# Tile sums of the Down projection made from whole SwiGLU tiles read back from DRAM, and two more paired slabs

## The chip, the cores and the metric

One core of a Trainium2 chip runs the kernel. The metric is device time in microseconds. The kernel before takes 1428.65 us (median of 3 runs, 1428.42 to 1428.69). Its parts: TensorE (PE) multiplies matrices and accumulates in PSUM; VectorE (DVE), ScalarE (ACT) and GpSimd (POOL) do the elementwise work; SyncE (SP) and POOL issue most of the DMA transfers between DRAM and the on-chip memory (SBUF). Each engine works through its own queue in order, so an instruction that waits holds up all that stands behind it on that engine.

## The reference

One encoder block on a sequence of 256 tokens with a model width of 2048, all in float32. The input is normalised and sent through four mixers, whose outputs go through one projection; cross-attention to 256 memory rows follows; then comes the SwiGLU feed-forward part, which is where the change lies:

```
x = x + mix @ w_out
x = x + cross_attention(rms_norm(x, norm_g[1]), mem_n, w_xq, w_xkv, w_xo)
def swiglu(h, w_gate_up, w_down):
    gate, up = jnp.split(h @ w_gate_up, 2, axis=-1)
    return (jax.nn.silu(gate) * up) @ w_down
x = x + swiglu(rms_norm(x, norm_g[2]), w_gate_up, w_down)
return rms_norm(x, final_norm_g)
```

The hidden width is 5632, that is 44 tiles of 128. `w_gate_up` is 2048 x 11264 and `w_down` 5632 x 2048.

## The kernel before

**Precision.** A float32 product is made of three matmuls in a faster format. Each operand is split into a high and a low half (`wh` and `wl` for weights, the two halves of a 512-wide tile for activations), and high x high, high x low and low x high are added up. `part` (lines 472 to 474) issues these three, each 512 columns wide. ScalarE makes the high half by a copy that rounds, VectorE the low half by a subtraction.

**Weights.** `Stream` reads the weights from DRAM in slabs of 128 x 2048 values, in the order of use. SyncE loads a slab into one of a few `raw` buffers; ScalarE and VectorE split it, in pieces ("halves"), into one of a few pairs `wh`/`wl`. In Down there are three `raw` buffers and four such pairs, so the split can run ahead of TensorE by some three pieces. `_plain` (lines 166, 167) splits a plain slab in two pieces of 1024. The splits of consecutive slabs keep their order by explicit dependencies.

**Paired slabs.** For some slabs (`S` in a plan string) the kernel uses Strassen's scheme as Winograd arranged it, on blocks of two tiles of the contracted dimension, two column blocks and the two halves of the rows: seven products in place of eight. A plain slab is 8 calls of `part`, a paired one 7. In return it needs sums of weights and sums of activations. `_sums` (lines 178, 179, 189) makes the weights' part: pieces of 1024, 512, 1024 and 1024, and between the second and the third either four additions of 512 on VectorE, or, for "summed" slabs, two, after SyncE has loaded a part, ScalarE has copied it (line 119) and a DMA from POOL that adds (line 121) has made the rest in one of the four `res` tiles. Only gate_up's paired slabs are summed. Down's make the four additions.

**Sums of activations.** `combine` makes, for a pair of activation tiles `a`, `b`, the sums of their row halves and splits them into a tile `z` (in Down: `y0` to `y7`). The tiles lie in SBUF in split form, so it first adds high and low halves again (two additions of 128 x 256), then makes four sums of 128 x 128, then splits them. In Down with its narrower `y` tiles the fourth sum overwrites the first tile of the pair. A pair's sums are made once; pass two uses those of pass one again.

**gate_up.** Eleven groups of 512 hidden columns. The first is plain; the plans `GROUPS` hold for the other ten: nine times `NSSNSSNN`, and `NSNSNSNN` for the last. After a group the SwiGLU product is transposed and stored by POOL to a DRAM tensor, `hidden` (`self.ff`; line 600). `load_turned` (line 605) loads a tile of it back in the arrangement that Down needs: 128 KB in runs of 128 bytes, issued by POOL. `fetch` loads tiles and splits them into `f`: 22 early ones during gate_up, the other 22 (`rest`, running six loads ahead of the splits) from the last group on. Tiles 20 to 27 of `f` lie in the buffers `z` of gate_up's own sums, tiles 28 to 43 in those of its input. At the end the `res` tiles, which held weight sums, get the residual back from DRAM (line 1230).

**Down.** Two passes over 22 slabs, each for two blocks of 512 output columns, with the plans `PASSES`. In pass one the plain slabs take `soon` tiles first. `ready(k)` drives the fetch so that the tile of a step is there, at a pace of three tiles in four steps. The generator `combined` calls `combine` for one pair after another; `before(j)` drives it, so that the sums of slab j have been issued when slab j begins. `mixed` and `done` add the products to the residual; `mixed` uses a 128 x 512 tile `u`. The last 12 steps are held back for `down_end`.

**Order.** `Background` is a planner at build time. Generators such as `fetch` and `combined` do a piece and yield a pause; `poll`, called after every part, resumes those whose pause has passed on a clock that counts 0.68 us for a part, but only while the planner's tally of VectorE's debt (`owed`) is under 0.9 us. The debt is added to the pause. `keep_place` ties an instruction to its place on its engine's queue.

Of the kernel before, what the change touches and what calls it, by code (L numbers as in the profile page):

```python
# [49 lines left out]
PAIRED = {a + i for a, plan in [(GATE_UP + 8 * j, GROUPS[j % len(GROUPS)]) for j in range(10)] + [(DOWN, PASSES[0]), (DOWN + 22, PASSES[1])]  # L50
          for i, x in enumerate(plan) if x in "Ss"}
AHEAD = (-3, -3)

SUMS = [{GATE_UP + 8 * j + i + a: GATE_UP + 8 * j + i for j in range(10) for i, x in enumerate(GROUPS[j % len(GROUPS)]) if x == "S"}
        for a in AHEAD]

SUMMED = {GATE_UP + 8 * j + i for j in range(10) for i, x in enumerate(GROUPS[j % len(GROUPS)]) if x == "S"}

# [18 lines left out]
class Stream:  # L77


    def __init__(self, tc, pools, W, bg):  # L80
        self.tc, self.nc, self.W, self.bg = tc, tc.nc, W, bg
        self.rawp, self.wp = pools
        self.order = []
        self.n = self.made = 0
        self.after = []
        self.halves = []
        self.at = self.phase = 0
        self.raw = None
# [6 lines left out]
        self.begun = []  # L95

# [8 lines left out]
    def _load(self, n):  # L105
# [4 lines left out]
        self.raw = slot[0].tile([P, 2048], F32, name="raw", tag="raw")  # L110
        if n // 16 in SUMS[0]:
            t = self.sums[0]
            self.sums.append(self.sums.pop(0))
            nc.sync.dma_start(t[:, 0:512], self.W[SUMS[0][n // 16]][:, 1536:2048])
            self.begun.append(t)
        if n // 16 in SUMS[1]:
            t = self.begun.pop(0)
# [3 lines left out]
            nc.gpsimd.dma_start(t, self.W[SUMS[1][n // 16]][:, 512:1536], accum_op=ALU.add)  # L121
            self.two.append(t)
# [170 lines left out]
class Block:  # L293
# [563 lines left out]
    def whole(self, c):  # L857
        return self.res[c].rearrange("p k r -> p (k r)")

    def leave(self, c):  # L860
        self.nc.sync.dma_start(self.rd[:, c * 1024:(c + 1) * 1024], self.whole(c))
# [238 lines left out]
    def gate_up(self, gp, f, z):  # L1100
# [39 lines left out]
        def fetch(k0, k1, ahead, pause, after=0, slow=False):  # L1140

            m = {}
            for k in range(k0, k1 + ahead):
# [11 lines left out]
                if k >= k0 + ahead:  # L1155
                    while k0 == 0 and k - ahead >= 20 and "free" not in box:
                        yield
                    mark = self.mark()
# [47 lines left out]
        up(0, ps[1])  # L1206
        early = fetch(0, FT - 22, 2, 2.0, 12, True)
        self.bg.drain(comb)
        for j in range(1, DFF // 512):
            plan = GROUPS[(j - 1) % len(GROUPS)]  # L1210
            if j == 10:
                box["free"] = True
# [15 lines left out]
        more.close()  # L1228
        for c, x in enumerate(whole):
            nc.sync.dma_start(x, self.rd[:, c * 1024:(c + 1) * 1024])  # L1230
        for _ in early:
# [3 lines left out]
    def down(self, f, sp):  # L1235
# [8 lines left out]
        u = sp.tile([P, 512], F32, name="u")  # L1244
        sums = [((2 * i, 2 * i + 1), z[i % 8]) for i in range(PASSES[1].count("S"))]
# [41 lines left out]
        def ready(k):  # L1287

            need = min(FT, max(k + 3, FT - 22 + next(asked) * 3 // 4))
            while self.have < need:  # L1290
                self.bg.step(next(e for e in self.bg.q if e[0] is self.fetch))

        for i, plan in enumerate(PASSES):
            n = plan.count("S")
# [697 lines left out]
```

## Time and profile before

The profiled execution took 1428.43 us; its span from the first to the last instruction is 1426.6 us.

| | busy us | share of the span |
|---|---|---|
| TensorE matmul | 1416.5 | 99% |
| TensorE weight load | 1176.1 | 82% |
| VectorE | 1174.3 | 82% |
| ScalarE | 850.2 | 60% |
| POOL | 243.4 | 17% |

The granted TensorE clock is 0.999 of full speed over the span. The last gate_up group runs from about 1146 us to 1186 us of the span; Down's first pass begins at 1186.42 us, where TensorE first reads a tile `f`. Matmuls are pipelined: a record of 0.39 us begins before the one ahead of it ends, so the pitch from start to start tells the throughput, not the length.

### The profile page before, as it was taken

What the parts mean: (1) busy time and instruction counts of PE and PEld (TensorE: products, weight loads), DVE (VectorE), ACT (ScalarE), POOL (GpSimd) and SP (SyncE); (2) the same over time, 40 slices, a digit from 0 to 9 for tenths busy, and PEclk for the clock granted to TensorE, in tenths of its full rate; (3) what the DMA queues carried; (4) which work ended last, traced back from release to release, by engine and by line L of the source; (5) the groups of instructions that cost most, each with busy time, mean ns of one, the idle gap of its engine ahead of it and who ended that gap; (6) DMA issues with size and microseconds to landing.
All of it is one profiled execution on the core that took longest, in us unless ns stands there. A gap on an engine that the chain in (4) does not pass through costs nothing.

```text
span 1426.6 us, 18663 instructions
## 1 busy us (share of the span) xinstructions
PE 1416.5 (99%) x6562; PEld 1176.1 (82%) x6562; DVE 1174.3 (82%) x1782; ACT 850.2 (60%) x1242; POOL 243.4 (17%) x315
## 2 busy tenths in 40 slices
PE   9999999999999999999999999999999999999997
PEld 8888888888888888888888888888888888788886
DVE  6667868787878767677578999999999988989997
ACT  7566665445755555555465676667666665655655
POOL 0000100003212233531331121122211024000000
PEclk9999999999999999999999999999999999999999
DMA  9886554457566797965798999999999898665554
GB/s 356 294 291 250 204 198 174 161 177 232 183 216 215 234 278 249 276 197 188 252 298 257 265 280 283 288 291 260 278 291 273 276 276 242 212 235 179 193 220 148
DMA packets 72462, 344.84 MB, mean 242 GB/s; under 512 B 10894, under 2 KB 12591, under 8 KB 45745
## 3 DMA queue, kind: packets, MB, share of 16 engines
q1 hardware_dynamic: 52976, 285.31, 57.4%
q0 software_dynamic: 18960, 57.69, 17.2%
q8 instruction: 51, 0.84, 0.2%
q10 hardware_dynamic: 432, 0.66, 0.1%
q14 instruction: 43, 0.34, 0.1%
HBM read 321.07 MB, written 22.54 MB: 241 GB/s over the span
## 4 chain that ended last, share of the span: by engine, by line
PE 92%; issue 3%; DVE 2%; DMA 2%; POOL 1%; ACT 0%; SPq 0%; DVEq 0%; ACTq 0%; POOLq 0%
PE pg L472 21%; PE pg L474 21%; PE pg L473 21%; PE pm L473 6%; PE pm L474 6%; PE pm L472 6%; PE pg L420 4%; PE pg L421 2%; PE pm L1445 1%; DMA raw<-in_W 1%; PE pm L1074 1%; DMA tmp<-hidden 1%; POOL tmp L605 1%; PE pm L1045 1%; DVE wl L179 0%
## 5 line engine op out<-in xcount | busy, mean ns | idle before, releaser
L167 DVE TENSOR_TENSOR wl<-raw,wh 128x1024 fp32r<-128x1024 f32 (+1 forms) x395 | 473.7, 1212 | 161.3 <-ACT wh L166 159.4
L166 ACT CAST wh<-raw 128x1024 fp32r<-128x1024 f32 (+1 forms) x395 | 406.4, 1042 | 253.0 <-PE pg L474 189.0
L472 PE MATMUL pg<-wh,act 128*128 128x512 f32 (+1 forms) x1165 | 455.5, 391 | 0.0
L474 PE MATMUL pg<-wh,act 128*128 128x512 f32 (+1 forms) x1165 | 453.9, 390 | 0.5 <-DVE act L322 0.5
L473 PE MATMUL pg<-wl,act 128*128 128x512 f32 (+1 forms) x1165 | 453.6, 389 | 0.2 <-DVE wl L167 0.2
L474 PEld LDWEIGHTS pg<-wh,act 128*128 128x128 f32 x1165 | 218.9, 188 | 47.0 <-DVE act L322 1.1
L472 PEld LDWEIGHTS pg<-wh,act 128*128 128x128 f32 x1165 | 219.0, 188 | 46.8 <-issue 1.5
L473 PEld LDWEIGHTS pg<-wl,act 128*128 128x128 f32 x1165 | 219.0, 188 | 45.1 <-DVE wl L167 0.5
L178 ACT CAST wh<-raw 128x1024 fp32r<-128x1024 f32 (+1 forms) x177 | 161.5, 918 | 158.8 <-DVE raw L189 62.7
L179 DVE TENSOR_TENSOR wl<-raw,wh 128x1024 fp32r<-128x1024 f32 (+1 forms) x177 | 182.7, 1057 | 25.7 <-ACT wh L178 24.3
L473 PE MATMUL pm<-wl,act 128*128 128x512 f32 x290 | 112.9, 389 | 0.2 <-DVE wl L167 0.2
L472 PE MATMUL pm<-wh,act 128*128 128x512 f32 x290 | 112.8, 389 | 0.0
L474 PE MATMUL pm<-wh,act 128*128 128x512 f32 x290 | 112.8, 389 | 0.0
L420 PE MATMUL pg<-act,wh 128*128 128x512 f32 x256 | 90.5, 395 | 0.0
L121 POOL DMA_DIRECT2D res<-in_W x39 | 35.0, 897 | 238.3 <-ACT res L119 211.1
L421 PE MATMUL pg<-act,wl 128*128 128x256 f32 x256 | 71.8, 280 | 0.0
L189 DVE TENSOR_TENSOR raw<-raw 128x512 f32<-128x512 f32 x99 | 68.2, 689 | 1.6
L473 PEld LDWEIGHTS pm<-wl,act 128*128 128x128 f32 x290 | 54.4, 188 | 11.8 <-DVE wl L167 0.5
L474 PEld LDWEIGHTS pm<-wh,act 128*128 128x128 f32 x290 | 54.4, 188 | 11.3
L472 PEld LDWEIGHTS pm<-wh,act 128*128 128x128 f32 x290 | 54.4, 188 | 11.3
L420 PEld LDWEIGHTS pg<-act,wh 128*128 128x128 f32 x256 | 48.1, 188 | 10.5
L178 ACT CAST wh<-res 128x1024 fp32r<-128x1024 f32 x39 | 41.2, 1055 | 14.8 <-PE pg L474 4.1
(376 smaller groups left out, 1933.0 us busy)
## 6 DMA issues: line engine op xcount, KB each, us to landing
raw<-in_W SPq DMA_DIRECT2D x207, 1024.0 KB, 5.5
raw<-in_W SPq DMA_DIRECT2D x39, 768.0 KB, 8.9
res<-in_W POOLq DMA_DIRECT2D x39, 512.0 KB, 9.7
res<-in_W SPq DMA_DIRECT2D x39, 256.0 KB, 4.9
raw<-in_W SPq DMA_DIRECT2D x11, 512.0 KB, 7.1
hidden<-g POOLq DMA_DIRECT2D x22, 256.0 KB, 4.0
tmp<-hidden POOLq DMA_DIRECT2D x44, 128.0 KB, 10.5
features<-tmp POOLq DMA_DIRECT2D x32, 128.0 KB, 4.6
```

Source lines behind the costliest of these rows:

```text
L121: nc.gpsimd.dma_start(t, self.W[SUMS[1][n // 16]][:, 512:1536], accum_op=ALU.add)
L166: nc.scalar.copy(wh[:, a:b], r[:, a:b])
L167: nc.vector.tensor_tensor(out=wl[:, a:b], in0=r[:, a:b], in1=wh[:, a:b].bitcast(F32), op=ALU.subtract)
L178: nc.scalar.copy(wh, src)
L179: nc.vector.tensor_tensor(out=wl, in0=src, in1=wh.bitcast(F32), op=ALU.subtract)
L189: nc.vector.tensor_tensor(out=out, in0=a, in1=b, op=ALU.add)
L420: self.nc.tensor.matmul(p[:, :], wh, slot[:, :], start=start, stop=False)
L421: self.nc.tensor.matmul(p[:, 0:R], wl, slot[:, 0:R], start=False, stop=stop)
L472: self.nc.tensor.matmul(p, hi, wh, start=start, stop=False)
L473: self.nc.tensor.matmul(p, hi, wl, start=False, stop=False)
L474: self.nc.tensor.matmul(p, lo, wh, start=False, stop=stop)
L605: self.nc.gpsimd.dma_start(t.rearrange("p (g t) -> p g t", t=32), src)
```

## The change

- Down's `combine` no longer adds the split halves. For each pair two DMAs from POOL load the whole tiles from `hidden` into the two halves of `u`, and `combine` reads those. `u` holds one pair at a time: the loads of a pair are issued when the pair before is combined, and the generator then pauses 10 us on the planner's clock. The first loads of a pass are issued as it begins. `combine` needs two temporary tiles, not four.
- `before(j)` asks for the sums of the pair of slab j+1 when slab j begins, so a plain slab lies between.
- The plans: the last gate_up group is like the others (four pairs, not three), and pass one of Down has seven pairs, not six, the first at slabs 5 and 7 (were 5 and 8). Down's paired slabs are now spelled `s`; as before they are not summed by DMA.
- As the last group now uses all four `z`, 20 tiles are fetched early, not 22, and 24 in `rest`, which runs seven loads ahead, starts one step earlier in the last group, and is paced by five tiles in eight steps. Pass one's `soon` tiles are 14 to 19 (were 12 to 19).
- `begins` replaces the table `SUMS`; with these plans it gives each sum the same place, three slabs ahead. `fetch_rows` is the loop of line 1230 under a name.

```diff
+EARLY = 20
-GROUPS = *["NSSNSSNN"] * 9, "NSNSNSNN"
+GROUPS = "NSSNSSNN",
-PASSES = "NNNNNSNNSNNSNSNNSNNSNN", "NSNSNSNSNSNSNSNSNSNNNN"
+PASSES = "NNNNNsNsNNsNsNNsNsNsNN", "NsNsNsNsNsNsNsNsNsNNNN"
...
+def begins():
+    at = {}
+    ns = sorted(SUMMED)
+    for i, n in enumerate(ns):
+        a = max(n - 3, ns[i - 4] + 1) if i >= 4 else n - 3
+        assert a not in at and a < n, (a, n)
+        at[a] = n
+    return at
...
-    def combine(self, z, a, b):
-        tt, t, u, v, w = self.tt, *(self.tmp() for _ in range(4))
-        for x, y in ((t, a), (u, b)):
-            tt(x, y[:, 0:R].bitcast(F32), y[:, R:512].bitcast(F32), ALU.add)
-        yield SOON
+    def combine(self, z, a, b, whole=None):
+        tt = self.tt
+        if whole:
+            t, u, v, w = *whole, self.tmp(), self.tmp()
+        else:
+            t, u, v, w = (self.tmp() for _ in range(4))
+            for x, y in ((t, a), (u, b)):
+                tt(x, y[:, 0:R].bitcast(F32), y[:, R:512].bitcast(F32), ALU.add)
+            yield SOON
...
-        early = fetch(0, FT - 22, 2, 2.0, 12, True)
+        early = fetch(0, EARLY, 2, 2.0, 12, True)
...
-                rest = fetch(FT - 22, FT, 6, SOON, slow=True)
+                rest = fetch(EARLY, FT, 7, SOON, slow=True)
...
-                if j == 10 and i > 2:
+                if j == 10 and i > 1:
                     next(rest)
...
         def combined(n):
-            for ks, x in sums[len(made):n]:
-                yield from self.combine(x, *(f[k] for k in ks))
+            whole = [u[:, a:a + R] for a in (0, R)]
+            todo = sums[len(made):n]
+            def load(ks):
+                mark = self.mark()
+                for y, k in zip(whole, ks):
+                    self.load_turned(y, self.ff, k)
+                self.keep_place(mark)
+            load(todo[0][0])
+            yield 10.0
+            for i, (ks, x) in enumerate(todo):
+                yield from self.combine(x, *(f[k] for k in ks), whole)
                 made.append(x)
-                yield 2.0
+                if i + 1 < len(todo):
+                    load(todo[i + 1][0])
+                    yield 10.0
...
-            need = min(FT, max(k + 3, FT - 22 + next(asked) * 3 // 4))
+            need = min(FT, max(k + 3, EARLY + next(asked) * 5 // 8))
...
-            g = self.bg.add(combined(n))
+            g = self.bg.add(combined(n), go=True)
...
             def before(j):
-                while plan[j] == "S" and len(made) <= plan[:j].count("S"):
+                while len(made) < sum(x in "Ss" for x in plan[:j + 2]):
                     self.bg.step(next(e for e in self.bg.q if e[0] is g))
...
-                                        () if i else range(2 * n, 2 * n + 8))
+                                        () if i else range(2 * n, EARLY))
```

More of the change, by code (lines that the diff above doesn't have):

```diff
@@ L42 @@
 LATE = 12
+EARLY = 20
 GATE_UP = 1920 // 16 + 8
-GROUPS = *["NSSNSSNN"] * 9, "NSNSNSNN"
+GROUPS = "NSSNSSNN",
 DOWN = GATE_UP + 80
-PASSES = "NNNNNSNNSNNSNSNNSNNSNN", "NSNSNSNSNSNSNSNSNSNNNN"
[L50 to L57, printed above, removed]
+PASSES = "NNNNNsNsNNsNsNNsNsNsNN", "NsNsNsNsNsNsNsNsNsNNNN"
+PLANS = [(GATE_UP + 8 * j, GROUPS[j % len(GROUPS)]) for j in range(10)] + [(DOWN, PASSES[0]), (DOWN + 22, PASSES[1])]
+PAIRED, SUMMED = ({a + i for a, plan in PLANS for i, x in enumerate(plan) if x in kinds} for kinds in ("Ss", "S"))
+def begins():
[6 more added lines that the diff above has]
+    return at
+SUMS = begins()
 LAG, OWED, SOON, FAR = 1.3, 0.9, 0.01, 18.0
@@ L94, in __init__ @@
         self.two = []
-        self.begun = []
     def _buffers(self, n, m):
@@ L110, in _load @@
         self.raw = slot[0].tile([P, 2048], F32, name="raw", tag="raw")
-        if n // 16 in SUMS[0]:
+        if n // 16 in SUMS:
             t = self.sums[0]
             self.sums.append(self.sums.pop(0))
[L114 to L117, printed above, removed]
+            nc.sync.dma_start(t[:, 0:512], self.W[SUMS[n // 16]][:, 1536:2048])
             mark = len(nc.cur_bb.bb.instructions)
@@ L120, in _load @@
             self.keep(mark)
-            nc.gpsimd.dma_start(t, self.W[SUMS[1][n // 16]][:, 512:1536], accum_op=ALU.add)
+            nc.gpsimd.dma_start(t, self.W[SUMS[n // 16]][:, 512:1536], accum_op=ALU.add)
             self.two.append(t)
@@ L858, in whole, with fetch_rows @@
         return self.res[c].rearrange("p k r -> p (k r)")
+    def fetch_rows(self, cs):
+        for c in cs:
+            self.nc.sync.dma_start(self.whole(c), self.rd[:, c * 1024:(c + 1) * 1024])
     def leave(self, c):
@@ L1155, in fetch @@
                 if k >= k0 + ahead:
-                    while k0 == 0 and k - ahead >= 20 and "free" not in box:
-                        yield
                     mark = self.mark()
@@ L1228, in gate_up @@
         more.close()
-        for c, x in enumerate(whole):
-            nc.sync.dma_start(x, self.rd[:, c * 1024:(c + 1) * 1024])
+        self.fetch_rows(range(4))
         for _ in early:
@@ L1244, in down @@
         u = sp.tile([P, 512], F32, name="u")
-        sums = [((2 * i, 2 * i + 1), z[i % 8]) for i in range(PASSES[1].count("S"))]
+        sums = [((2 * i, 2 * i + 1), z[i % 8]) for i in range(sum(x in "Ss" for x in PASSES[1]))]
         made, split = [], []
         def combined(n):
-            for ks, x in sums[len(made):n]:
-                yield from self.combine(x, *(f[k] for k in ks))
+            whole = [u[:, a:a + R] for a in (0, R)]
[9 more added lines that the diff above has]
+                yield from self.combine(x, *(f[k] for k in ks), whole)
                 made.append(x)
-                yield 2.0
+                if i + 1 < len(todo):
+                    load(todo[i + 1][0])
+                    yield 10.0
         def squares(x, c, r):
@@ L1293, in down @@
         for i, plan in enumerate(PASSES):
-            n = plan.count("S")
-            g = self.bg.add(combined(n))
+            n = sum(x in "Ss" for x in plan)
+            g = self.bg.add(combined(n), go=True)
             late = (0, LATE)[i]
```

2 lines of the change are left out of this document (removed).

## The prediction

> **What bounds the kernel now.** I read the page first (busy times, chain), then TensorE's waits, then a table of stretches, then the timelines around the two places where TensorE stops.
>
> ```profile
> span 1426.6 us, 18663 instructions
> PE 1416.5 (99%) x6562; PEld 1176.1 (82%) x6562; DVE 1174.3 (82%) x1782; ACT 850.2 (60%) x1242; POOL 243.4 (17%) x315
> PE 92%; issue 3%; DVE 2%; DMA 2%; POOL 1%; ACT 0%; SPq 0%; DVEq 0%; ACTq 0%; POOLq 0%
> ```
>
> TensorE is busy in 99% of the span and carries 92% of the chain that ended last. A shorter time needs fewer matmuls, or fewer stops. This is all that TensorE waits for:
>
> ```profile
> PE pm L643 <- DVE eps L644: 1.1, 1, 1.1
> PE pg L474 <- DVE act L322: 0.5, 1, 0.5
> PE pm L472 <- ACT y L338: 0.2, 1, 0.2
> PE pg L473 <- DVE wl L167: 0.2, 1, 0.2
> PE pm L473 <- DVE wl L167: 0.2, 1, 0.2
> ```
>
> Only the first row lies outside the stages that the change touches: it is the start. The next view is the table of stretches; its columns are the stretch and its length, then busy time with instruction counts for PE, PEld, DVE, ACT and POOL, the granted clock, the DMA share and GB/s. The first row is ordinary gate_up groups, the second the last group, and Down's first pass runs from 1186 to about 1301.
>
> ```profile
> 900.00:1000.00 100.00, 100.00 (x443) 82.81 (x442) 96.35 (x119) 66.12 (x82) 20.13 (x23) 1.00 0.94 280
> 1146.00:1186.00 40.00, 40.00 (x179) 33.10 (x178) 33.86 (x39) 22.62 (x26) 6.96 (x8) 1.00 0.87 259
> 1186.00:1213.00 27.00, 27.00 (x121) 22.36 (x120) 22.25 (x36) 14.96 (x25) 15.57 (x18) 1.00 0.89 241
> 1213.00:1241.00 28.00, 27.27 (x119) 21.86 (x118) 27.27 (x51) 18.40 (x29) 0.88 (x1) 1.00 0.74 241
> 1241.00:1270.00 29.00, 29.00 (x130) 24.01 (x129) 28.93 (x56) 16.30 (x26) 0.00 (x0) 1.00 0.55 207
> 1270.00:1301.00 31.00, 31.00 (x139) 25.66 (x138) 26.07 (x36) 17.11 (x20) 0.00 (x0) 1.00 0.48 172
> ```
>
> VectorE is the second bound: 22.25 + 27.27 + 28.93 + 26.07 = 104.5 us of the 115 of pass one, and nearly all of 1213 to 1270. That TensorE loses so little shows that the split weights lie ahead of it in their buffers. A new stop therefore comes from VectorE or ScalarE falling behind by more than that lead.
>
> **Step 1: two products fewer.** Counted from the strings, pair slabs go from 9x4 + 3 + 6 + 9 = 54 to 40 + 7 + 9 = 56. A plain slab is 8 parts of three matmuls, a pair slab 7. The pitch of a part:
>
> ```profile
> 1186.42 0.39 PE L472 MATMUL pg<-wh,f 128*128 128x512 f32 x1
> 1188.46 0.39 PE L472 MATMUL pg<-wh,f 128*128 128x512 f32 x1
> ```
>
> These are the first matmuls of parts 1 and 4 of Down: 2.04 us for three parts, 0.68 each (0.39 is the pipelined length of one). Two parts are **-1.36 us**, certain as long as TensorE stays the bound. Plain and pair slabs then take 5.44 and 4.76 us.
>
> **Step 2: the stops that a late combination makes.** The two stops of the first pass:
>
> ```profile
> 1214.98 0.48 PE L472 MATMUL pg<-wh,act 128*128 128x512 f32 x1
> 1215.71 0.47 PE L472 MATMUL pm<-wh,y 128*128 128x512 f32 x1 [0.25 <-ACT y L338]
> 1231.46 0.39 PE L474 MATMUL pg<-wh,act 128*128 128x512 f32 x1
> 1232.33 0.50 PE L474 MATMUL pg<-wh,act 128*128 128x512 f32 x1 [0.48 <-DVE act L322]
> 1232.67 0.40 PE L472 MATMUL pm<-wh,y 128*128 128x512 f32 x1
> ```
>
> Both wait for results of `combine` (`y`, and its fourth sum, written back into `act`): slab 5 and slab 8, the first two pair slabs. The starts should be 0.227 apart, so they cost 0.50, and 0.64 + 0.11, some **1.27 us** with the matmul behind the first stop. Now `before(j)` asks for the pair of slab j+1 before slab j begins, so these results are a plain slab early. I take -1.27; the ends are 0 and -1.27. The two stops late in pass two (0.2 each in the waits) stand where no combination is made, so I leave them; at best they go too, 0.4.
>
> **Step 3: VectorE's sum.** The durations, from the groups of VectorE between 1186 and 1301:
>
> ```profile
> L179 DVE TENSOR_TENSOR wl<-raw,wh 128x1024 fp32r<-128x1024 f32 x18 | 22.0, 1221 | 4.2 <-ACT wh L178 4.1
> L189 DVE TENSOR_TENSOR raw<-raw 128x512 f32<-128x512 f32 x24 | 16.5, 687 | 0.2
> L322 DVE TENSOR_TENSOR act<-tmp,act 128x256 fp32r<-128x256 f32 x16 | 6.4, 420 | 0.6 <-ACT act L330 0.6
> L322 DVE TENSOR_TENSOR tmp<-tmp 128x128 f32<-128x128 f32 x24 | 6.2, 285 | 0.1
> L179 DVE TENSOR_TENSOR wl<-raw,wh 128x512 fp32r<-128x512 f32 x6 | 4.1, 688 | 1.1 <-ACT wh L178 1.1
> ```
>
> A pair slab in Down is 3 x 1.22 + 0.69 + 4 x 0.69 = 7.1 us, a plain one 2 x 1.22 = 2.44. A combination was 2 x 0.42 (the adds now gone) + 4 x 0.285 + 0.42 + 2 x 0.285 = 3.0; it becomes 2.1. Pass one: one more pair slab +4.7, 6 x 3.0 becoming 7 x 2.1 = -3.3, two more tiles to split (24 for 22) +0.84, so +2.2: 106.7 of 114.3 us, 93%. The mean has room. Pass two makes two combinations in place of three: 9.0 becomes 4.2, no cost. In the last group a summed pair slab has two adds: 3 x 1.22 + 0.69 + 2 x 0.69 = 5.7 for 2.44, so 33.9 + 3.3 = 37.2 of 39.3, the 95% at which the groups of 900 to 1000 run without a stop: 0. Its added SyncE and POOL loads and ScalarE copy are those of one more such slab, as in the groups before; it ends, like them, in two plain slabs. All four residual tiles now wait for that group's sums, so on SyncE one reload more may stand ahead of weight loads, as this one does without TensorE stopping: 0.
>
> ```profile
> 1168.74 0.33 SPq L1230 DMA_DIRECT2D res<-residual  x1
> 1206.15 0.43 DVE L322 TENSOR_TENSOR act<-tmp,act 128x256 fp32r<-128x256 f32 x1 [0.56 <-ACT act L330]
> ```
>
> Locally it is tighter. The first pair slabs are 5 and 7 (were 5 and 8), with one plain slab between. The second row is VectorE's last idle gap before the stops, 20 us into Down. Slab 7 starts at 5 x 5.44 + 4.76 + 5.44 = 37.4, and its last sum is read 3.4 later, at 40.8. In the 20.8 us between, VectorE owes two pair slabs, one plain, combination 1 and some five tile splits: 14.2 + 2.4 + 2.1 + 2.1 = 20.8. Back-to-back instructions overlap a little, so the isolated durations overstate. The margin is that of a pair-plain-pair run in pass two:
>
> ```profile
> 1330.62 1.23 DVE L179 TENSOR_TENSOR wl<-raw,wh 128x1024 fp32r<-128x1024 f32 x1
> 1332.92 0.39 PE L473 MATMUL pm<-wl,act 128*128 128x512 f32 x1
> ```
>
> The low half of the pair slab's last sum ends at 1331.85, TensorE reads it at 1332.92: 1.07 us. A combination of 2.1 us inside such a run overdraws it by at most 1.0. In the old first pass a 3.0 us combination beside slabs 11 and 13 cost nothing (no wait there). I take **+0.5** for slab 7, +0.2 for slabs 12, 17 and 19 together; ends 0 and 4 x 1.0.
>
> **Step 4: eighteen new loads on POOL.** Nine pairs need two whole tiles each from `hidden` into the two halves of `u`. The rows of the like loads, in POOL's timeline, the source's landing times and ScalarE's timeline:
>
> ```profile
> 1191.20 7.03 POOL L605 DMA_DIRECT2D tmp<-hidden  x8
> 1209.07 0.88 POOL L605 DMA_DIRECT2D tmp<-hidden  x1 [0.94 <-DVE act L322]
> 1215.10 0.88 POOL L605 DMA_DIRECT2D tmp<-hidden  x1 [5.15 <-DVE tmp L322]
> DMA to landing us min/median/max: 5.2/10.6/13.1
> 1198.20 0.41 ACT L330 CAST z<-tmp 128x256 fp32r<-128x256 f32 x1 [2.37 <-DMA tmp<-hidden]
> ```
>
> The first pair's loads go ahead of the tile loads and push them back by 2 x 0.88 = 1.76 us. ScalarE already waits 2.37 there at no cost to TensorE, and one more tile is loaded early in the last group (six for five), so 0. The first combination reads 10 us and VectorE's debt after its loads are emitted; POOL is free for them at 1191.2, 5 us into Down, and a first load there lands 7 us on (1191.20 to 1198.20), while VectorE is idle in part: 0. Pair 1 is the delicate one: its loads stand behind a dozen tile loads, which come in one per some 1.4 us (the first at 1198.20, the sixteenth, issued at 1209.07, at about 1219.7 by the median). As loads 15 and 16 they land 32 to 34 us into Down. VectorE wants them at 32 to 33: the demand falls before slab 6, 5 x 5.44 + 4.76 = 32.0 in. Its subtract blocks VectorE in order: behind it wait the low halves of slab 7, and TensorE for those. I take +0.2, as the two instants nearly meet; ends 0 and +7 (all tile loads ahead of it: the old ones are in at 1215.10 + 5.2 = 1220.3, five more make 1226 to 1227, 40 us into Down and 7 late). Later pairs load alone; the one old load so placed (1215.10) is at the minimum, 5.2, so with 1.76 of issue they fit into 10: 0. A POOL load into `u` waits for the subtracts before it; behind it wait tile loads, seven tiles ahead of use now.
>
> [...]
>
> **The sum.** -1.36 - 1.27 + 0.7 + 0.2 = -1.73. The profiled execution took 1428.43 (span 1426.6 and 1.8 around it), 0.22 below the median of 1428.65; to the median I forecast **1426.9 us**, -0.12%. About 0.2% (2.9 us) is what a measurement of this kernel can tell from no change.
>
> **Rivals.** *A: every stop goes.* Both stops of step 2 and the two late ones go (-1.36 - 1.27 - 0.4), nothing new: 1425.6. For it: pass two has one combination less and 5 us less VectorE work. Against: the late stops lie beside the final additions, not beside a combination.
>
> *B: VectorE stops TensorE at each pair-plain-pair.* Slabs 7, 12, 17 and 19 lose 1.0 each: 1428.65 - 2.63 + 4.0 = 1430.0, the saving given back. For it: the margin of 1.07, and VectorE at 93% in the mean. Against: the old slabs 11 and 13.
>
> *C: the tiles come late for every pair.* If the loads keep the crowded landing time of 10.6 even after the fetch is over, each pair is 10.6 + 1.76 - 10 - 1.07 = 1.3 us late at TensorE, and six pairs make 7.8: 1428.65 - 2.63 + 7.8 = 1433.8, slower by 0.36% (the end of +7 in step 4 would give 1433.5 with the 0.5 of step 3). It decides against the kernel from a landing time of about 10.2 on (5.5 us over six pairs). Against it stands the 5.2 of the lone load. [...]
>
> *D: the parts are saved but not felt*, because VectorE already sets the pace. The page has TensorE at 99% against 82%; it could only be so inside pass one, which is B.
>
> **How the numbers follow.** My forecast 0.50 (its own range 1425.8 to 1428.2), A 0.12, B with D 0.23, C 0.15. The range, 1425.4 to 1431.0, holds all but C and a few hundredths of the tails of A and B. Faster by over 0.2% (below 1425.8) is most of A: 0.10. Slower (above 1431.5) is C and the tail of B: 0.16. Within: 0.74.
>
> **What would show it.** Lines 472 to 474 hold two matmuls fewer each. No TensorE wait on `y` or `act` near 1215 and 1232; the late ones still there. POOL has 18 loads `u<-hidden` and no idle of 5 us before its last tile load. VectorE is 2 us busier in pass one and 5 less in pass two. A VectorE wait on the load into `u` just before slab 7 is my delicate place; one before every pair, with TensorE waiting on `wl`, is C and would make the prediction wrong. Stops at slabs 7, 12, 17 and 19 with no wait on a load are B.

## The result, and the profile after

The changed kernel takes 1442.05 us (median; 1441.5 to 1442.7). The kernel before, run beside it, takes 1428.67 us (1428.42 to 1429.41). The ratio is 1.0093, with a 95% interval of 1.0075 to 1.011. The forecast of 1426.9 us is wrong, in sign and by more than its range: the kernel is slower by 13.4 us.

The profiled execution took 1442.7 us. First the top of its page, with busy times by engine and the chain's shares:

```profile
span 1440.9 us, 18712 instructions
PE 1420.9 (99%) x6556; PEld 1177.2 (82%) x6556; DVE 1176.9 (82%) x1774; ACT 854.0 (59%) x1247; POOL 259.9 (18%) x334
PE 94%; DMA 2%; DVE 1%; issue 1%; POOL 1%; ACT 0%; SPq 0%; DVEq 0%; POOLq 0%; ACTq 0%
```

Six matmuls fewer (6556 for 6562) are the two products saved. Yet TensorE is "busy" 4.4 us longer: its matmuls take longer somewhere. What TensorE waits for (total, times, longest):

```profile
PE pg L478 <- DVE wl L184: 3.8, 1, 3.8
PE pg L479 <- DVE act L327: 3.3, 1, 3.3
PE pm L477 <- ACT wh L183: 2.0, 1, 2.0
PE pm L478 <- DVE wl L184: 1.1, 1, 1.1
```

These four rows are new, and all are paired-slab work (L184 and L183 split the pieces of a paired slab, L327 is the two-input operation of `combine` and of the tile splits). The table of stretches tells where, with the same columns and stretches as before:

```profile
1146.00:1186.00 40.00, 40.00 (x178) 33.12 (x177) 36.08 (x41) 24.69 (x27) 7.84 (x9) 1.00 0.94 292
1186.00:1213.00 27.00, 27.00 (x121) 22.34 (x120) 18.55 (x32) 13.20 (x23) 16.44 (x19) 1.00 0.88 262
1213.00:1241.00 28.00, 21.14 (x83) 16.42 (x82) 23.20 (x38) 14.91 (x23) 7.05 (x8) 0.88 0.64 184
1241.00:1270.00 29.00, 25.68 (x101) 20.41 (x100) 23.04 (x44) 15.32 (x26) 4.40 (x5) 0.88 0.47 163
1270.00:1301.00 31.00, 30.98 (x137) 25.19 (x136) 29.01 (x45) 17.20 (x24) 1.76 (x2) 1.00 0.65 239
```

Nearly all of the loss lies in the third and the fourth row, slabs 5 to 12 of Down's first pass: 83 and 101 matmuls where there were 119 and 130. The last gate_up group, with its fourth pair, is full (40.00 of 40). VectorE is not overloaded in the two bad stretches: it does less than before (23.20 for 27.27, 23.04 for 28.93). It stands still. Its timeline (start, length, instruction, and in brackets the idle time before it and what ended that):

```profile
1209.76 0.41 DVE L327 TENSOR_TENSOR act<-tmp,act 128x256 fp32r<-128x256 f32 x1
1217.51 0.49 DVE L327 TENSOR_TENSOR tmp<-u 128x128 f32<-128x128 f32 x2 [7.34 <-DMA u<-hidden]
...
1218.45 0.68 DVE L184 TENSOR_TENSOR wl<-raw,wh 128x512 fp32r<-128x512 f32 x1
...
1247.74 0.29 DVE L327 TENSOR_TENSOR tmp<-u 128x128 f32<-128x128 f32 x1 [3.32 <-DMA u<-hidden]
```

For 7.34 us VectorE stands at the second pair's tiles, and for 3.32 us at the fourth's. Queued behind is the second piece of slab 5's weights (128x512), which was due long before that pair's sums are. TensorE's timeline, around the two places:

```profile
1215.03 0.39 PE L477 MATMUL pg<-wh,act 128*128 128x512 f32 x1
1219.19 0.50 PE L478 MATMUL pg<-wl,act 128*128 128x512 f32 x1 [3.77 <-DVE wl L184]
...
1221.88 0.80 PE L477 MATMUL pm<-wh,y 128*128 128x512 f32 x1 [1.96 <-ACT wh L183]
1223.80 0.80 PE L478 MATMUL pm<-wl,y 128*128 128x512 f32 x1 [1.13 <-DVE wl L184]
1224.39 0.63 PE L479 MATMUL pm<-wh,y 128*128 128x512 f32 x1
1224.82 0.63 PE L477 MATMUL pm<-wh,y 128*128 128x512 f32 x1
...
1252.04 1.22 PE L479 MATMUL pg<-wh,act 128*128 128x512 f32 x2 [3.31 <-DVE act L327]
1253.06 0.63 PE L477 MATMUL pm<-wh,act 128*128 128x512 f32 x1
```

The stops are 3.77, 1.96 and 1.13 us, and then 3.31. Behind them the starts lie 0.43 us apart (1224.39 to 1224.82), where 0.227 is usual, though nothing is waited for. Two short stretches around the end of the first such stretch show the granted clock (the last column but two):

```profile
1223.80:1227.00 3.20, 3.20 (x8) 2.55 (x9) 3.20 (x5) 2.19 (x3) 1.90 (x3) 0.50 0.65 143
1227.00:1231.00 4.00, 4.00 (x19) 3.32 (x18) 3.93 (x6) 1.32 (x3) 0.00 (x0) 0.99 0.92 326
```

So these stops are paid for twice: as idle time, and as matmuls at a granted clock of 0.50 for 3.2 and 5.7 us behind them. The stretches at half rate, 1223.80 to 1226.95 and 1252.04 to 1257.75, lose half of their 8.9 us, some 4.4 us. Added up over all matmuls after 1000 us, the part of the pitch above 0.227 us (pitches over 0.3 us counted) is 16.9 us, where it was 2.1 before. The difference of 14.8, less the 1.36 of the saved products, is 13.4 of the 14.3 us by which the span grew. Of the last 0.9, some 0.7 is lost in the first 24 us of the span, before anything that was changed: TensorE waits 0.52 us there at 13.32, which it did not before.

Why the tiles came so late shows in POOL's timeline, which issues the loads:

```profile
1196.20 1.77 POOL L614 DMA_DIRECT2D u<-hidden  x2 [4.96 <-ACT z L335]
1197.97 8.76 POOL L614 DMA_DIRECT2D tmp<-hidden  x10
1207.02 0.88 POOL L614 DMA_DIRECT2D tmp<-hidden  x1 [0.29 <-issue]
1208.07 1.75 POOL L614 DMA_DIRECT2D u<-hidden  x2 [0.17 <-DVE y L327]
...
1242.04 0.88 POOL L614 DMA_DIRECT2D u<-hidden  x1 [4.73 <-DVE tmp L327]
```

The first pair's loads were held up 4.96 us, since `u`'s memory was still in use by gate_up. Eleven tile loads went ahead of the second pair's, and VectorE was at the reader at 1210.17, 2.1 us after the first of the pair's two loads was issued. It had to wait for nearly the whole journey of the loads. The second of the fourth pair's loads, at 1242.04, itself waited until the third pair had read `u`, and VectorE was at the fourth pair's reader by 1244.4. The times from issue to landing of all eighteen loads, in the view of the tile `u`:

```profile
DMA to landing us min/median/max: 2.8/4.0/8.6
```

The longest, 8.6 and 8.4 us, are the second pair's, behind the tile loads; the fourth pair's took 5.2 and 5.6.

### The profile page after: what moved, and what is told of

It reads as the page before. It is cut to its first block, busy times and chain, and to the rows that moved or that the text cites. A ratio compares the mean times of both kernels' runs of the same rounds, so it can differ in the third digit from the quotient of the medians.

```text
span 1440.9 us, 18712 instructions
## 1 busy us (share of the span) xinstructions
PE 1420.9 (99%) x6556; PEld 1177.2 (82%) x6556; DVE 1176.9 (82%) x1774; ACT 854.0 (59%) x1247; POOL 259.9 (18%) x334
## 4 chain that ended last, share of the span: by engine, by line
PE 94%; DMA 2%; DVE 1%; issue 1%; POOL 1%; ACT 0%; SPq 0%; DVEq 0%; POOLq 0%; ACTq 0%
PE pg L479 21%; PE pg L477 21%; PE pg L478 21%; PE pm L478 7%; PE pm L477 7%; PE pm L479 7%; PE pg L425 4%; PE pg L426 2%; DMA u<-hidden 1%; PE pm L1468 1%; PE pm L1088 1%; DMA raw<-in_W 1%; PE pm L1059 1%; DMA tmp<-hidden 0%; PE pm L1877 0%
## 5 line engine op out<-in xcount | busy, mean ns | idle before, releaser
L183 ACT CAST wh<-raw 128x1024 fp32r<-128x1024 f32 (+1 forms) x184 | 167.9, 918 | 168.4 <-DVE raw L194 76.6
L184 DVE TENSOR_TENSOR wl<-raw,wh 128x1024 fp32r<-128x1024 f32 (+1 forms) x184 | 189.8, 1057 | 28.2 <-ACT wh L183 26.7
L477 PE MATMUL pm<-wh,act 128*128 128x512 f32 x284 | 110.7, 390 | 0.0
L479 PE MATMUL pm<-wh,act 128*128 128x512 f32 x284 | 110.7, 390 | 0.0
L194 DVE TENSOR_TENSOR raw<-raw 128x512 f32<-128x512 f32 x104 | 71.5, 688 | 2.0
L183 ACT CAST wh<-res 128x1024 fp32r<-128x1024 f32 x40 | 42.2, 1055 | 15.1 <-PE pg L479 4.2
```

Of the source, the lines that this page charges most:

```text
L183: nc.scalar.copy(wh, src)
L184: nc.vector.tensor_tensor(out=wl, in0=src, in1=wh.bitcast(F32), op=ALU.subtract)
L194: nc.vector.tensor_tensor(out=out, in0=a, in1=b, op=ALU.add)
L477: self.nc.tensor.matmul(p, hi, wh, start=start, stop=False)
L479: self.nc.tensor.matmul(p, lo, wh, start=False, stop=stop)
```

## The experiments

The theory after the profile: `combine`'s four reads of `u` (lines 492 to 495 of the changed kernel) are not tied to their place, while the loads are, by `keep_place`. They are issued after slab 7's first piece. The build's scheduler, as I read it, knows nothing of a load's journey, so it moves them up VectorE's queue, ahead of slab 5's second piece, and VectorE, which works in order, stands there, for 7.34 us at the second pair. The rivals: the loads themselves (their traffic, POOL's queue) cost the time; the new plans do; or VectorE's sum is too tight (rival B).

**Tie the readers.**

```diff
+        mark = self.mark()
         tt(v[:, 0:P], t[:, P:R], u[:, P:R], ALU.subtract)
 ...
         tt(w[:, P:R], u[:, 0:P], v[:, P:R], ALU.add)
+        if whole:
+            self.keep_place(mark)
         yield SOON
```

> The changed kernel with one difference: the four subtractions and additions of combine that read the loaded tiles are tied to their place on VectorE's queue, so that the build's scheduler cannot put them ahead of weight splits that were issued before them. Theory 1 (the subtraction was moved up the queue and blocks it): the 7.3 us and 3.3 us waits of VectorE on the load into u go, TensorE's stops near 1215 to 1223 and 1248 with them; 1427 us, 1425.8 to 1429. Theory 2 (the loads themselves come too late for slab 7, wherever the reader stands): VectorE still waits over 3 us before slab 7 and TensorE stops; 1433 or more. Theory 3 (pair-plain-pair at slabs 5 and 7 overdraws VectorE): no wait on a load, but TensorE waits for wl at 7, 12, 17 and 19; 1430 to 1433.

Measured: 1433.24 us (1431.68 to 1434.88), ratio to before 1.003 (1.002 to 1.0041). Some 9 of the 13.4 us come back, and the waits go as theory 1 says, but its 1427 us is missed by 6. VectorE's timeline around the second pair:

```profile
1219.07 1.22 DVE L184 TENSOR_TENSOR wl<-raw,wh 128x1024 fp32r<-128x1024 f32 x1
1220.21 0.49 DVE L327 TENSOR_TENSOR tmp<-u 128x128 f32<-128x128 f32 x2
```

No bracket stands behind the reader: the tiles are there. At its place of issue it comes at 1220.21, 34 us into Down and behind six more pieces of weights; the scheduler had put it at 1210.2. What TensorE still waits for:

```profile
PE pm L478 <- DVE wl L184: 1.0, 2, 0.8
PE pg L477 <- ACT act L343: 0.7, 1, 0.7
```

Still 4 us slower than before, with no wait of VectorE on a pair's load left. So a second cost exists.

**Make the tiles by additions into `u`, with no load.** In place of the two loads, each half of `u` gets its tile by one addition of the split halves on VectorE; all else is the changed kernel.

```diff
-                    self.load_turned(y, self.ff, k)
-                self.keep_place(mark)
+                    self.tt(y, f[k][:, 0:R].bitcast(F32), f[k][:, R:512].bitcast(F32), ALU.add)
```

> The changed kernel with its plans, its slab of lead and its holder u, but the two whole tiles of a pair are made by two additions of high and low halves on VectorE, not loaded. Theories 1 and 2: no VectorE wait on a DMA, all stops over 1 us gone; 1427 us, up to 1429 for 6 us more of VectorE work in pass one. Theory 3: 1430 to 1433, no better than a pinned version with loads.

Measured: 1430.71 us (1429.91 to 1431.51), ratio 1.0011 (1.0001 to 1.0021). The readers are untied here too, and nothing waits for a journey, so the early reader does no harm of that size without the load. The expected 1427 to 1429 us is missed all the same, and it is not a clean measurement: the first write into `u` waits 2.44 us on VectorE for gate_up's store (the same memory), and TensorE stops for 1.42 us near 1216. The next but one experiment does without `u`.

**The loads alone, in the kernel before.** The new `combine` and `combined` with their loads, put into the kernel before with its old plans and its old demand.

```diff
-                yield from self.combine(x, *(f[k] for k in ks))
+            load(todo[0][0])
+            yield 10.0
+            for i, (ks, x) in enumerate(todo):
+                yield from self.combine(x, *(f[k] for k in ks), whole)
                 made.append(x)
-                yield 2.0
+                if i + 1 < len(todo):
+                    load(todo[i + 1][0])
+                    yield 10.0
...
-            g = self.bg.add(combined(n))
+            g = self.bg.add(combined(n), go=True)
```

> The kernel before with the loads alone: old plans, old demand (a pair's sums when its own slab begins), old fetch; combine reads two loaded tiles in place of making the two additions. Theory 1: the subtraction is again moved up the queue; VectorE waits for u 3 to 8 us before slab 8 and TensorE loses 3 to 8 us: 1431 to 1437. Theory 3 (the plans cost, not the loads): 1427 to 1429. If it is above the changed kernel's 1442, the slab of lead was worth something.

Measured: 1439.15 us (1438.54 to 1439.9), ratio 1.0071 (1.0056 to 1.0086): 10.1 us slower with the loads, and the `combine` that reads them, as the only edit, and more than the 1431 to 1437 us of theory 1. VectorE at the second pair's reader (two later pairs make it wait another 2.01 and 1.98 us); then the costliest of TensorE's waits:

```profile
1222.13 0.29 DVE L322 TENSOR_TENSOR tmp<-u 128x128 f32<-128x128 f32 x1 [4.26 <-DMA u<-hidden]
```

```profile
PE pg L473 <- DVE wl L179: 4.6, 2, 4.4
```

**The change without the loads.** The new plans, the lead of a slab and the fourth pair in the last group, with the old `combine` on the kernel's own tiles (and the fetch six ahead and begun one step later, as before).

```diff
...
-                yield from self.combine(x, *(f[k] for k in ks), whole)
+                yield from self.combine(x, *(f[k] for k in ks))
                 made.append(x)
-                if i + 1 < len(todo):
-                    load(todo[i + 1][0])
-                    yield 10.0
+                yield 2.0
...
```

> The change without its loads: new plans, the slab of lead, 20 tiles early, but combine adds the halves into its own temporary tiles as before, and the fetch runs six tiles ahead, not seven (the tiles do not reach further). It has no write into u, which in e2_adds waited 2.4 us for memory still in use and pushed slab 5's weight load back. If the plans are sound (step 1 and 2 of the prediction): 1426.5 to 1427.5. If seven pairs in pass one overdraw VectorE (theory 3): 1429 to 1432, with TensorE waits on wl or act at slabs 5, 7 or 10.

Measured: 1428.74 us (1428.19 to 1429.71), ratio 0.9997 (0.9988 to 1.0007): no change. So the whole loss comes with the loads, and the rest of the change gains nothing that can be told. The saved 1.36 us and the two old stops do not show, since TensorE has new stops a little later:

```profile
PE pm L477 <- ACT wh L183: 0.6, 1, 0.6
PE pg L479 <- DVE act L327: 0.4, 2, 0.2
```

They stand at 1236.6 to 1252.5, where the old kernel had none. The excess of the pitch is 3.2 us here and 2.1 before, so 1.1 of the 1.36 us are given back. This kernel still makes the additions that the loads were to save, 7 x 0.84 = 5.9 us of VectorE in pass one, and VectorE (the third busy time) has no room left from 1213 to 1301, where it had 5.7 us before (82.27 of 88 busy):

```profile
1213.00:1301.00 88.00, 87.00 (x379) 70.00 (x377) 87.01 (x147) 54.34 (x79) 5.27 (x6) 1.00 0.59 205
```

What the plans would gain with the additions saved and every load in time, no run shows.

**The lead alone, and the fourth pair alone,** each in the kernel before.

```diff
-                while plan[j] == "S" and len(made) <= plan[:j].count("S"):
+                while len(made) < plan[:j + 2].count("S"):
```

> The kernel before with the slab of lead alone: a pair's sums are demanded when the slab before it begins; old plans, old combine, no loads. Step 2 of the prediction says that the stops at slabs 5 and 8 (0.50 and 0.75 us) go: 1427.4, 1427 to 1428. If the place of issue does not matter because the scheduler moves combine anyway: 1428.7. If the earlier combination delays the weight split instead: 1429 to 1430.

```diff
-GROUPS = *["NSSNSSNN"] * 9, "NSNSNSNN"
+GROUPS = "NSSNSSNN",
...
-        early = fetch(0, FT - 22, 2, 2.0, 12, True)
+        early = fetch(0, 20, 2, 2.0, 12, True)
...
```

> The kernel before with four pairs in the last gate_up group alone (20 tiles early, the other 24 at the old pace, six ahead); Down as before. One part less: 1428.0 (-0.68) if the last group has room, as step 3 said; 1429 or more if the two extra fetches in Down or the lost lead at Down's start cost TensorE a stop.

Measured: 1429.04 us (1428.67 to 1430.11), ratio 1.0001 (0.9992 to 1.0011), and 1429.40 us (1428.61 to 1430.47), ratio 1.0003 (0.9993 to 1.0012). With the lead the stop near 1215 goes, and one of 0.87 us at 1232, on `wl`, comes in its place; with the fourth pair two of 0.28 and 0.53 us at 1218 and 1219 come in Down. Neither alone makes a difference that can be measured.

**Two pairs loaded ahead, readers tied.** In pass one `y7`, free until then, holds every other pair, so that a load need not wait until the pair before has been read.

```diff
-            whole = [u[:, a:a + R] for a in (0, R)]
+            both = [[x[:, a:a + R] for a in (0, R)] for x in ((u, z[7].bitcast(F32)) if n < 9 else (u,))]
...
-                if i + 1 < len(todo):
-                    load(todo[i + 1][0])
+                if i + m < len(todo):
+                    load(i + m)
```

> The pinned version with two holders in pass one (the second is the tile y7, which pass one does not use), so that a pair's loads are issued one pair earlier. Theory 1: as e1_pin within 0.5 us, since no load is waited for there. Theory 2: better than e1_pin by 3 us or more. Both: POOL's first four loads push the tile loads back by 3.5 us, ScalarE waits for tiles that much longer, no cost to TensorE.

Measured: 1435.54 us (1435.09 to 1436.27), ratio 1.0046 (1.0031 to 1.0061): not better than one holder (1433.24), which neither theory has. Four pair loads now stand ahead of the tile loads. ScalarE waits 6.90 us at 1207.66 for a tile, where its longest such wait in the changed kernel's pass one is 2.48, and TensorE, to which this was to cost nothing, stops from 1210 on. POOL's queue, at 0.88 us for an issue, is a second bound here: earlier for one kind of load is later for the other.

**The pair loads on ScalarE's queue, readers tied.**

```diff
-                    self.load_turned(y, self.ff, k)
+                    src = self.ff[k * R:(k + 1) * R, :].rearrange("(g f) (b t) -> (f b) g t", f=32, t=32)
+                    nc.scalar.dma_start(y.rearrange("p (g t) -> p g t", t=32), src)
```

> The pinned version with the pair loads issued from ScalarE's queue, not POOL's, so that they do not stand behind eleven tile loads. Theory 2 (the queue position and the late landing are what costs): better than e1_pin by 2 us or more, 1429 to 1431. Theory 1 (the order on VectorE's queue was the cost): no better than e1_pin, 1432 to 1434; ScalarE may lose 1 to 5 us at Down's start, where the first load waits for memory, and TensorE with it.

Measured: 1442.04 us (1441.79 to 1443.22), ratio 1.0092 (1.0077 to 1.0107). Both theories are missed. Issued from 1196.30 on beside POOL's tile loads, the first pair arrives after all of those that stand around it, as the view of `u` (landing, for the ten of the eighteen loads that the trace follows) and VectorE's timeline show:

```profile
DMA to landing us min/median/max: 2.4/3.4/20.9
```

```profile
1217.80 0.49 DVE L327 TENSOR_TENSOR tmp<-u 128x128 f32<-128x128 f32 x2 [9.63 <-DMA u<-hidden]
```

The wait is now on the first pair, at its right place, and longer than the changed kernel's (9.63 us for 7.34). That the time is the changed kernel's is chance.

**Tie the second pair only.** `keep_place` as above, for the pair of slab 7 alone.

```diff
+        if tied:
+            self.keep_place(mark)
...
-                yield from self.combine(x, *(f[k] for k in ks), whole)
+                yield from self.combine(x, *(f[k] for k in ks), whole, n == 7 and len(made) == 1)
```

> The changed kernel with the reads of u tied to their place of issue for the second pair alone, all others left to the build. Theory (each wait of VectorE has its own price at TensorE, idle and half rate together): the wait of 7.34 us goes, and with it stops of 3.77 + 1.96 + 1.13 us and some 2 us of half rate, so 1442.05 - 8.9 = 1433.2 (1432 to 1435); the wait of 3.32 us at 1248 and the half rate behind it stay. Rival (the lateness belongs to the loads and goes to the next pair when one is mended): the third pair's wait grows to 6 or more, and the time stays above 1438.

Measured: 1433.23 us (1432.25 to 1436.59), ratio 1.0035 (1.0021 to 1.0048). This one pair was worth some 9 us, as worked out from the stops behind its wait and their half rate. The fourth pair's wait stays, a little smaller, the sixth's takes the place of the seventh's, and none grows to 6 us:

```profile
1241.70 0.29 DVE L327 TENSOR_TENSOR tmp<-u 128x128 f32<-128x128 f32 x1 [2.69 <-DMA u<-hidden]
...
1270.20 0.29 DVE L327 TENSOR_TENSOR tmp<-u 128x128 f32<-128x128 f32 x1 [2.09 <-DMA u<-hidden]
```

**Tie pass one only.**

```diff
+                yield from self.combine(x, *(f[k] for k in ks), whole, n == 7)
```

> The changed kernel with the four reads of u tied to their place of issue in pass one alone; pass two is left to the build. Theory (early readers of pass one are the loss, and the late stops of the kernel with all readers tied come from tying pass two's): 1431.8 us, 1431 to 1433; no VectorE wait on u in pass one, TensorE's stops at 1394 and 1404 to 1406 back to one of about 0.2. Rival (the late stops come from something else, and tying pass two costs nothing): 1433.2, with the stops at 1394 to 1406 still there.

Measured: 1432.45 us (1431.03 to 1433.62), ratio 1.0024 (1.0012 to 1.0035). Against 1.003 with all tied this can't be told apart. The stop at 1394 is gone; those behind 1404 are 0.21, 0.31 and 0.07 in place of 0.47, 0.27 and 0.07. In pass one, where both tie the same readers, this trace has a stop of 1.06 us near 1216 that the other has not. The small question stays open.

**The stop by itself.** The kernel before, with one useless reduction on VectorE where the changed kernel's VectorE stands.

```diff
+                if not i and j == 4:
+                    mark = self.mark()
+                    nc.vector.memset(u, 0.0)
+                    nc.vector.tensor_reduce(out=u[:, 0:1], in_=u[:, None, :].to_broadcast([P, 14, 512]), op=ALU.add, axis=mybir.AxisListType.XY)
+                    self.keep_place(mark)
```

> The kernel before, with one useless reduction of 14 x 512 elements put on VectorE ahead of slab 5's second piece of weights, where the changed kernel's VectorE stands still; no load and no plan is changed. An estimate from VectorE's rows (1.22 us for 1024 elements, 0.69 for 512) is 7.5 to 8.5 us for it. Theory (a stop of VectorE of this length is enough, whatever makes it): TensorE is idle some 6 to 8 us after it, and then takes about 0.43 us for a matmul in place of 0.23 for a dozen or more of them, so 1429.1 + 8 to 10 = 1437 to 1439. Rival (the half rate and part of the idle time belong to the loads and their traffic): idle time alone, no matmuls at 0.43, at most 1435.

Measured: 1436.87 us (1436.36 to 1437.67), ratio 1.0057 (1.0043 to 1.007): 8.0 us for 8.1 us of VectorE (7.61 for the reduction, 0.49 for the `memset` before it), with no load and no plan changed. VectorE, then TensorE, then two stretches with the clock:

```profile
1209.43 7.61 DVE L1307 TENSOR_REDUCE u<-u 128x1 f32<-128x7168 f32 x1
1216.95 0.68 DVE L179 TENSOR_TENSOR wl<-raw,wh 128x512 fp32r<-128x512 f32 x1
```

```profile
1217.69 0.51 PE L473 MATMUL pg<-wl,act 128*128 128x512 f32 x1 [2.67 <-DVE wl L179]
1221.62 0.79 PE L472 MATMUL pg<-wh,act 128*128 128x512 f32 x1 [2.99 <-ACT wh L178]
1222.57 0.79 PE L472 MATMUL pg<-wh,z 128*128 128x512 f32 x1 [0.15 <-ACT wh L166]
```

```profile
1222.50:1228.00 5.50, 5.43 (x12) 3.98 (x13) 4.55 (x12) 0.92 (x4) 0.88 (x1) 0.50 0.56 173
1228.00:1234.00 6.00, 6.00 (x27) 4.88 (x27) 4.91 (x6) 4.91 (x7) 0.00 (x0) 0.98 0.54 191
```

TensorE stops in the same slab, for 2.67 + 2.99 + 0.15 = 5.8 us, and then 5.5 us pass at a clock of 0.50. So the half rate belongs to the stop, not to the loads or their traffic, and a stop of VectorE here is passed on to the end nearly one for one.

**The plans without loads, first pairs a slab later** (slabs 6, 9, 11 and 13 for 5, 7, 10 and 12), as a way to keep the saved products.

```diff
-PASSES = "NNNNNsNsNNsNsNNsNsNsNN", ...
+PASSES = "NNNNNNsNNsNsNsNsNsNsNN", ...
```

> The new plans without the loads (tile sums from the kernel's own tiles, as before), and pass one's first pairs a slab later: slabs 6, 9, 11, 13, 15, 17 and 19 in place of 5, 7, 10, 12, 15, 17 and 19. Theory (the stops of 0.23, 0.57 and 0.19 at 1236 to 1252 come from the two pairs at 5 and 7 beside the tile splits): they go, and the saved 1.36 us are seen in part, 1427.8 (1427.2 to 1428.4). Rival (VectorE is at its limit wherever the pairs stand): the stops move to slabs 11 to 15, 1428.7 or more.

Measured: 1431.35 us (1430.56 to 1432.15), ratio 1.0017 (1.0008 to 1.0026), as the rival has it and not the theory. The stops move and grow, among them these rows of TensorE's waits:

```profile
PE pg L477 <- ACT wh L183: 1.2, 3, 0.4
PE pg L479 <- DVE act L327: 0.9, 1, 0.9
```

They stand from 1234 to 1281, at slabs 9 to 17, in what is now a row of six pairs with one plain slab between each. VectorE has no room for such a row:

```profile
1234.00:1301.00 67.00, 64.76 (x278) 51.13 (x277) 66.76 (x114) 41.27 (x59) 0.00 (x0) 1.00 0.51 188
```

It is busy for 66.76 of the 67 us, ScalarE for 41.27. This is rival B's condition, though in a kernel that still makes the additions. No kernel of these is faster than the one before.

## Why the prediction was wrong

**Step 4 failed, at one sentence:** "VectorE wants them at 32 to 33: the demand falls before slab 6". That is where the combination is *issued*. The tied kernel puts its reader there, at 34 us into Down, and nothing waits. In the changed kernel the reader stood in VectorE's queue at 24 us. I took the order of issue for the order of the queue, for instructions that nothing ties. The trace of before had the answer, in rows of VectorE's timeline that I did not read:

```profile
1206.61 0.42 DVE L322 TENSOR_TENSOR tmp<-act 128x256 f32<-128x256 f32 x1
1207.10 1.23 DVE L179 TENSOR_TENSOR wl<-raw,wh 128x1024 fp32r<-128x1024 f32 x1
...
1208.70 0.43 DVE L322 TENSOR_TENSOR tmp<-act 128x256 f32<-128x256 f32 x1
```

The rows of 128x256 are the additions of slab 5's combination, 20 and 22 us into Down. The first stands ahead of slab 5's first piece of weights (1207.10). In the tied kernel a combination asked for as slab 6 begins stands behind slab 7's first piece. This one is asked for as slab 5 begins, or at least not before slab 4 does, since asking then (the lead alone) moves it to 1202.99. So the scheduler, it seems, moved this work forward in the old kernel too. There no load had to land for it, as all its inputs lay in SBUF.

The rest of step 4: that the loads would land "32 to 34 us into Down" was close (the wait ended at 1217.51, 31 us in). That POOL is free for the first loads at 1191.2 was wrong: they went at 1196.20. The claim "later pairs load alone, they fit into 10" failed for the fourth pair (3.32 us of wait) and the seventh (1.2 us, at 1281), since a load waits for the reader before it and the next reader is early again. The landing of a lone load, put at 5.2 us, was measured at 2.8 to 5.6 from the third pair on; the loads of the fourth and the seventh, for which VectorE waited, took 5.2 to 5.6. A row nearer to the shortest of these would not have saved the forecast, as the second pair's loads took 8.6 and 8.4 us beside the tile loads.

The upper end of +7 for this step is the size of what came at the second pair (3.77 + 1.96 + 1.13 = 6.9 us of idle), though for another reason than the one given (tile loads ahead). The stop of 3.31 us at the fourth pair and the half rate, some 4.4 us, were in no case of the prediction.

**Step 1** was right as a count (six matmuls), but the time isn't seen even without the loads. **Step 2** was right that the stops on `y` at 1215 and on `act` at 1232 go; it was wrong that -1.27 follows, since new stops at 1232 (lead alone) or 1236 to 1252 (plans without loads) take their place. "What is late next" was not asked there. Of the two stops of 0.2 us that the step puts late in pass two, one lies at 9.69 us, near the kernel's start; only that at 1403.00 is late. **Step 3**: the last group was right (36.08 of 40 us busy in its stretch, no stop; forecast 37.2 of 39.3). For pass one the +0.7 looks too small. Without loads the pitch loses 2.4 us there, all of it in new stops, where the old ones cost 1.34; -1.36 - 1.34 + 2.4 is -0.3, as measured (1428.74 beside 1429.06), and too little to be told from nothing. But that kernel still makes the additions, so no run shows the term as it was meant. That back-to-back instructions of VectorE overlap a little shows in the rows: two of 128x128 on `u` take 0.49 us, one 0.29.

**The rivals.** C had the sign and a price of 1433.8, but on slow landing at every pair, which only the second pair had; tying the readers removes every wait of VectorE on them with much the same landings (2.7 to 6.2 us, median 4.1). B is seen in the plans without loads, in small, and with the pairs a slab later, both with VectorE full. A did not occur. D, "parts saved but not felt", is nearest to the measured 0.9997 of the plans without loads. **What would show it** named a VectorE wait on the load into `u` just before slab 7; it was there, but in slab 5, and the chance I gave to a slower kernel, 0.16, left out the scheduler altogether.

**What stays open.** With the readers tied the loads still cost some 4.5 us against the plans without them (1433.24 and 1428.74). The two traces lie only 3.3 us apart (spans of 1429.9 and 1426.6), as the tied kernel's is of its fastest run, 1431.68. The excess of TensorE's pitch, 6.2 for 3.2 us, places 3.0 of these at small stops on weight pieces and on `act`, about half of them in pass one and half at the end of pass two. In pass one ScalarE waits up to 2.7 us for raw weights, where it waited at most 1.5 before and 1.1 without the loads, so crowding of the loads is likely, but no run takes it apart.

## What to carry to other kernels

Before a result of VectorE is replaced by a load, find in the trace of before where its reader really stands on its engine, not where the code issues it. Here VectorE reached such a reader early, and everything queued behind it, the weights of a paired slab two places earlier among it, waited 7.34 us for the rest of the load's journey; tie the reader as firmly as the load, and count what is queued ahead of the load on its own queue. Where the spare room was about 1 us (1.07 in the trace of before), 1.1 of the 1.36 us of the saved products were soon eaten by the next stops, so ask of each stop removed what is late next.

## What was not expected of the hardware

Behind its longer stops TensorE's matmuls ran 0.427 us apart in place of 0.227. Such stops were those of 3.77 us (with 1.96 and 1.13 after it) and 3.31 us in the changed kernel, 4.37 us with the loads alone, 2.77 us with only the second pair tied, and 2.67 and 2.99 us with the useless reduction. Behind single stops of 0.8 to 1.4 us, as in the tied kernel and with the additions into `u`, there was no such stretch: the mean granted clock of both spans is 0.999, as before.

The granted clock was 0.50 for 6.8 us twice in the changed kernel (1220.2 to 1227.1 and 1251.0 to 1257.8). With the useless reduction it was some 10.2 us, an estimate from the mean clocks of three stretches: 0.72 over the 7.9 us from 1214.6, 0.50 over the next 5.5, and 0.98 over the 6.0 behind them make 4.4 + 5.5 + 0.2. The half rate does not begin at one point of a stop. In the changed kernel it began 1.0 us after the stop of 3.77 us had ended, and the second time 2.2 us into the stop of 3.31. With only the second pair tied the matmuls behind the stop of 2.77 us at first still took 0.39 to 0.40 us; the longer ones, of 0.49 and then 0.63 to 0.71, begin at 1245.86, 1.3 us after the stop had ended. What sets the beginning and the length, no run shows.

A load of 128 KB issued from ScalarE's queue at 1196.30 took 20.9 us to land beside a run of POOL's tile loads. The median of the ten such loads that the trace follows was 3.4 us.
